# The first eight heads of a hybrid decoder block with queries on partitions, on one core

## The chip, the core and the metric

The kernel runs on one core of a Trainium2 chip. The core has five engines that each work through a queue of their own in order: TensorE (PE: matrix products, with a separate row PEld for loading its stationary operand), VectorE (DVE), ScalarE (ACT), GpSimd (POOL) and SyncE (SP), which here only issues transfers. The transfers of all queues run on 16 DMA engines. SBUF has 128 partitions; TensorE writes to PSUM, which has eight banks of 128 x 512 float32. The metric is the time of one execution on the device in microseconds.

## The reference, cut to what is computed

One decoder layer over 2048 tokens of width 1024, all in float32. A projection of the normed input gives queries, keys and values of eight heads of 64, and two halves u and v of a gated unit. Attention mixes three causal patterns (window, dilation), merged by their softmax denominators:

```python
DILATED_PATTERNS = ((128, 1), (512, 4), (2048, 16))
q, k, v_a, u, v_s = jnp.split(rms_norm(x, pre_mix_norm) @ w_in, ...)
for window, dilation in DILATED_PATTERNS:
    o, lse = dilated_window_attention(q, k, v, window, dilation)   # softmax over keys t - j*dilation
o = sum(softmax(lses)[p] * outs[p])                                # the three patterns merged
sgu = gelu(u) * (tril(w_spatial) @ layer_norm(gelu(v_s)) + b)      # per chunk of 128 tokens and group of 64
y = concat(rms_norm(attn), rms_norm(sgu)) @ w_out
x = x + rms_norm(y);  x = x + rms_norm(swiglu_ffn(rms_norm(x)))
```

## The kernel before

Float32 products are made of three (or two) products of halves: each operand is split into a rounded part (`hi`, a cast on ScalarE) and the rest (`lo`, a subtraction on VectorE). The 2048 tokens are four blocks m of 512. Attention runs in two halves x = 0, 1 of 1024 query tokens, eight heads each ("the first eight heads" are the eight heads of x = 0). Work is written as Python generators whose steps are interleaved by `_merge` (L1265) at a fixed pace; from that program order, with priority offsets (`high_priority`), a scheduler with its own model of times fixes the order of each engine's queue and each wait when the kernel is built. Buffers come from pools: tiles with one tag share `bufs` slots, and a new tile waits until the last reader of the old one is done.

Stages, in order: input projection of keys, queries and values of blocks 0 and 1 (to 187 us in the trace); then `merge(w1, ..., heads(0), ...)` at L1357 runs the rest of the input projection (gated unit of blocks 0 and 1, all of blocks 2 and 3) beside the heads of x = 0 (to 693 us); then output projection and the first FFN beside the heads of x = 1 (to about 1500 us); then the rest.

Attention, as it is before for both halves. `stacks` (L554) loads queries and keys of a head, transposed (dims on partitions, hi and lo rows stacked) and copies the keys of the near pattern on GpSimd to another order. `scores` (L652) computes scores with keys on partitions and up to 512 (key block, query) columns per PSUM bank; the scores go through `psq`, a pool of two banks (L107) that the gating product, the transposes of the gated unit and of the input preparation use as well. VectorE adds a mask whose values also carry the multiplicity of patterns (L723, L725, L733), and `fold` keeps a running maximum `macc` over keys. When all eight banks of a head are done, `lanes` (L599) transposes `macc` in 32 x 32 blocks, reduces it and `mix` (L740) spreads it back over the partitions as `mb`. Then each bank gets a subtraction of `mb` (L806, L811), an exponential on ScalarE (L819), the split into `ph` and `pl` (L820, L821), a running sum `dacc`, and products with the values into two accumulating banks per pattern kind (`psv`, L796, L798). At the end `lanes` reduces `dacc`, its reciprocal goes through DRAM (`dd`) and comes back spread over partitions (`rb`), and the pair of heads is divided (L852) and stored in `aT`. The scores of the next head are interleaved with `mix` of this one.

`ip_again` (L384) loads the normed input of block 0 again on SP. `ip_gate` (L499) loads the split gating weights (`ws`, 1 MB) once per block, four times in all. `out_rows` (L873) ends an output projection: after the last bank it loads eight rows of tiles of the residual (`xr`, one tile in the stage beside the heads of x = 1), adds each, stores it, takes its square on ScalarE, and fetches the next `xr` into the tile just freed:

```python
        def row(i, r):                                            # L895
            v.scalar_tensor_tensor(yj, yj, r, xs[i], ALU.mult, ALU.add)
            self.dma(dst[j * P:(j + 1) * P, 512 * n:512 * n + 512], yj)
            fetch(i + ahead)
```

Of the kernel before, what the change touches and what calls it, by code (L numbers as in the profile page):

```python
# [10 lines left out]
F32 = mybir.dt.float32  # L11
# [36 lines left out]
def shape_constants():  # L48
    i = np.arange(P)
    d = i[None, :] - i[:, None]  # L50
    ln2 = 8.0 * np.log(2.0)

    def logmul(dl):
        m = ((dl >= 0) & (dl <= 128)).astype(int) + ((dl >= 0) & (dl % 4 == 0)).astype(int)
        return np.where(m == 0, NEG, np.where(m == 1, 0.0, ln2))

    m0, m1, m2 = (logmul(d + 128 * k) for k in range(3))
    q = np.arange(256)
    r, nq, ii = q // 64, (q // 32) % 2, q % 32
# [5 lines left out]
    fcol = np.repeat(freq, 16)[:, None]  # L65
    return np.ascontiguousarray(
        np.concatenate([m2, m2, m1, m2, m0, m0, m1, p1, tril, fcol], axis=1).astype(np.float32))

# [9 lines left out]
SU_AT = 1  # L78
XR = 1
PV_LAG = 1  # L80
GATE_LAG = 1
PV_BUF = 3
R1 = 1.2
R2 = 1.1
# [11 lines left out]
C_FREQ = 1280  # L96
C_W = 1281


class Body:  # L100
# [32 lines left out]
    def dma(self, out, in_):  # L133
        if out.dtype == F32R:
            out = out.bitcast(F32)
        if in_.dtype == F32R:
            in_ = in_.bitcast(F32)
        self.nc.sync.dma_start(out, in_)  # L138

    def rstd(self, ss, n, inv_n, eps, name, parts=P):  # L140
# [358 lines left out]
    def ip_gate(self, m):  # L499
# [49 lines left out]
    def attn_pools(self, pool):  # L549
        self.ap = pool  # L550
        self.cst = pool.tile([P, C_TRIL], F32, name="cst")
        self.dma(self.cst, self.t["consts"][:, 0:C_TRIL])
# [46 lines left out]
    def lanes(self, acc, op, name):  # L599
# [3 lines left out]
        oth = self.tiny.tile([P, 32], F32, name=name + "_o", tag="ln_o", bufs=2)  # L603
        tr = self.ap.tile([P, 1024], F32, name=name + "_t", tag="mt", bufs=1)
        v.transpose(tr, acc)
# [260 lines left out]


    def ff_pools(self, pool, apool, ypool, xr):


        self.fp, self.fa, self.yp, self.xr = pool, apool, ypool, xr

    def out_rows(self, m, n_k, load, ops, res, gain, dst, keep):  # L873
# [12 lines left out]
        todo = [(n, j) for n in range(2) for j in range(4)]  # L886
        ahead = self.xr[2]

# [43 lines left out]
    def out_proj(self, m):  # L932
        nc, t, v, pool = self.nc, self.t, self.nc.vector, self.fp
        ah = [self.fa.tile([P, TB], F32R, name="ah", tag="ah", bufs=KT) for _ in range(KT)]
        al = [self.fa.tile([P, TB], F32R, name="al", tag="al", bufs=KT) for _ in range(KT)]
        rb = pool.tile([P, TB], F32, name="rbw", tag="tmp", bufs=4)
        order = [4, 5, 6, 7, 0, 1, 2, 3]
        with self.tc.high_priority(HP_O):
            for kt in order:
                raw = pool.tile([P, TB], F32, name="araw", tag="tmp", bufs=4)  # L940
                if kt < 4:
# [29 lines left out]
    def ffn_up(self, m):  # L971
# [5 lines left out]
        for g in range(NFF // 2):  # L977
# [17 lines left out]
            def evac(b, ps, g=g, hold=hold):  # L995
                if b < 2:
                    s = pool.tile([P, TB], F32, name="sil", tag="tmp", bufs=4)
                    nc.scalar.activation(s, ps, AF.Silu)
# [17 lines left out]
    def ffn_down(self, m):  # L1016
# [4 lines left out]
        def load_d(k, n):  # L1021
            s = pool.tile([P, TB], F32, name="araw", tag="tmp", bufs=4)
            self.dma(s, self.fD[m][k])
# [280 lines left out]
def build(tc, t):  # L1304
    with ExitStack() as ctx:
# [5 lines left out]
        with tc.tile_pool(name="sp", bufs=1, side="right") as sp:  # L1311
# [12 lines left out]
            with tc.tile_pool(name="su2", bufs=1) as su:  # L1324
# [4 lines left out]
                         36))  # L1329
        atx = ExitStack()  # L1330
        at = atx.enter_context(tc.tile_pool(name="at", bufs=1, side="right"))
        b.attn_pools(at)
        b.sbufs = 12
        ssq = at.tile([P, 1024], F32, name="ssq")
        b.ssq = [ssq, ssq]

        def heads(x):
            st, pair = {}, {}
            yield from b.scores(x, 0, st)
            for h in range(NH):  # L1340
# [6 lines left out]
                for _ in ahead:  # L1347
                    yield
            yield from b.attn_norm(x)

        G = 8 + 2 * GATE_LAG
        g0 = b.ip_gate(0)
# [3 lines left out]
                   _merge(b.ip_qkv(3), 30, b.ip_gate(3), 2 * G))  # L1356
        merge(w1, 4 * 50 + 24 + 4 * G, heads(0), 175 * R1)  # L1357
        ipx.close()
        ffx, fax = ExitStack(), ExitStack()
        ff = ffx.enter_context(tc.tile_pool(name="ff", bufs=1, side="left"))  # L1360
        fa = fax.enter_context(tc.tile_pool(name="fa", bufs=1, side="left"))
        b.ff_pools(ff, fa, ff, (ff, "xr", 1))
        merge(chain(b.out_proj(0), b.out_proj(1), b.ffn_prep(0), b.ffn_up(0),
                    _merge(b.ffn_down(0), 49, b.ffn_prep(1), 12), b.ffn_up(1)), 269, heads(1), (8 * 29 + 1) * R2)
        atx.close()
        with tc.tile_pool(name="ob", bufs=1, side="right") as ob:
            b.ff_pools(ff, fa, ff, (ob, "xr", 8))
            drain(b.out_proj(2))
            b.ff_pools(ff, ob, ob, (ob, "xr", 8))
            drain(b.out_proj(3))  # L1370
# [3 lines left out]
        b.hp = hpx.enter_context(tc.tile_pool(name="hp", bufs=1, side="right"))  # L1374
        b.ff_pools(ff, None, ff, (ff, "tmp", 4))
        with tc.tile_pool(name="pp", bufs=1, side="right") as pp:
# [40 lines left out]
```

## Time and profile before

Three runs took 2468.97, 2476.92 and 2474.16 us, median 2474.16. The profiled execution took 2476.58 us; its span from the first to the last instruction is 2474.8 us at a mean granted TensorE clock of 0.963 of full speed.

| engine | busy us | share of the span | instructions |
|---|---|---|---|
| PE | 2281.4 | 92% | 10421 |
| PEld | 1863.8 | 75% | 10421 |
| DVE | 1770.1 | 72% | 3430 |
| ACT | 1169.1 | 47% | 2141 |
| POOL | 349.3 | 14% | 373 |

All 347,600 packets of data went through one queue, that of SP (474.76 MB). Busy shares are unions of the instructions' spans, so two that overlap count once; in groups by line the spans are added. "granted clock" is the share of the full 2.4 GHz that TensorE was given; 0.5 is its lower level of 1.2 GHz. Matmuls are pipelined: the spans of neighbours overlap, and the distance from start to start is what one costs.

### The profile page before, as it was taken

What the parts mean: (1) busy time and instruction counts of PE and PEld (TensorE: products, weight loads), DVE (VectorE), ACT (ScalarE), POOL (GpSimd) and SP (SyncE); (2) the same over time, 40 slices, a digit from 0 to 9 for tenths busy, and PEclk for the clock granted to TensorE, in tenths of its full rate; (3) what the DMA queues carried; (4) which work ended last, traced back from release to release, by engine and by line L of the source; (5) the groups of instructions that cost most, each with busy time, mean ns of one, the idle gap of its engine ahead of it and who ended that gap; (6) DMA issues with size and microseconds to landing.
All of it is one profiled execution on the core that took longest, in us unless ns stands there. A gap on an engine that the chain in (4) does not pass through costs nothing. (4 is left out here: it accounts for less than half of the span.)

```text
span 2474.8 us, 32763 instructions
## 1 busy us (share of the span) xinstructions
PE 2281.4 (92%) x10421; PEld 1863.8 (75%) x10421; DVE 1770.1 (72%) x3430; ACT 1169.1 (47%) x2141; POOL 349.3 (14%) x373
## 2 busy tenths in 40 slices
PE   7997969889886999999999999999979999999997
PEld 6776758768675878887777888787757778887886
DVE  5428678995799985868899734667767676675567
ACT  6425765664644653535545532555422233334443
POOL 0000000000000000000000000000054466561012
PEclk9998979999998999999999999999989999999999
DMA  7867767778776665446656435678466633326655
GB/s 233 303 211 255 222 188 221 233 230 245 245 229 198 180 186 151 137 145 207 204 160 195 134 112 161 216 230 264 148 213 228 210 107 107 107 98 217 204 175 199
DMA packets 347772, 476.84 MB, mean 193 GB/s; under 512 B 30768, under 2 KB 174672, under 8 KB 347088
## 3 DMA queue, kind: packets, MB, share of 16 engines
q1 hardware_dynamic: 347600, 474.76, 60.5%
q8 instruction: 82, 1.34, 0.2%
q14 instruction: 90, 0.74, 0.1%
HBM read 365.12 MB, written 109.52 MB: 192 GB/s over the span
## 5 line engine op out<-in xcount | busy, mean ns | idle before, releaser
L171 DVE TENSOR_TENSOR w_lo<-w_raw,w_hi 128x512 fp32r<-128x512 f32 x368 | 252.6, 689 | 178.1 <-ACT w_hi L170 169.7
L170 ACT CAST w_hi<-w_raw 128x512 fp32r<-128x512 f32 x368 | 227.1, 618 | 307.1 <-PE d L199 236.2
L199 PE MATMUL d<-al,w_hi 128*128 128x512 f32 x704 | 276.4, 393 | 0.0
L199 PE MATMUL d<-ah,w_hi 128*128 128x512 f32 x704 | 276.3, 393 | 0.0
L199 PE MATMUL d<-ah,w_lo 128*128 128x512 f32 x704 | 276.1, 392 | 0.0
L1160 PE MATMUL d<-th,w_lo 128*128 128x512 f32 x616 | 246.6, 400 | 18.8 <-DVE w_lo L1047 18.7
L1160 PE MATMUL d<-th,w_hi 128*128 128x512 f32 x616 | 246.9, 401 | 11.4 <-ACT w_hi L1046 11.4
L1160 PE MATMUL d<-tl,w_hi 128*128 128x512 f32 x616 | 246.9, 401 | 0.0
L1047 DVE TENSOR_TENSOR w_lo<-raw,w_hi 128x512 fp32r<-128x512 f32 x187 | 142.6, 802 | 68.8 <-ACT w_hi L1046 67.8
L1046 ACT CAST w_hi<-raw 128x512 fp32r<-128x512 f32 x187 | 107.0, 618 | 131.8 <-PE d L1246 78.4
L199 PE MATMUL d<-w_hi,hh 128*128 128x512 f32 x384 | 153.7, 407 | 9.3 <-DVE io L436 4.8
L1160 PEld LDWEIGHTS d<-th,w_lo 128*128 128x128 f32 x616 | 118.4, 192 | 51.5 <-DVE w_lo L1047 25.3
L199 PE MATMUL d<-w_lo,hh 128*128 128x512 f32 x384 | 154.2, 402 | 2.5 <-DVE w_lo L171 2.2
L199 PE MATMUL d<-w_hi,hl 128*128 128x512 f32 x384 | 152.6, 400 | 0.0
L199 PEld LDWEIGHTS d<-ah,w_lo 128*128 128x128 f32 x704 | 132.7, 188 | 26.3
L199 PEld LDWEIGHTS d<-al,w_hi 128*128 128x128 f32 x704 | 132.7, 188 | 25.8
L199 PEld LDWEIGHTS d<-ah,w_hi 128*128 128x128 f32 x704 | 132.7, 189 | 25.0
L818 POOL MEMSET ph<- 128x128 f32 x64 | 13.1, 205 | 978.1 <-PE pv L796 611.1
L1160 PEld LDWEIGHTS d<-th,w_hi 128*128 128x128 f32 x616 | 118.6, 193 | 39.5 <-ACT w_hi L1046 12.9
L199 PE MATMUL d<-w_hi,fh 128*128 128x512 f32 x352 | 140.3, 398 | 4.1 <-ACT fh L1013 3.8
L199 PE MATMUL d<-w_hi,fl 128*128 128x512 f32 x352 | 138.2, 395 | 1.9 <-DVE fl L1014 1.9
L1160 PEld LDWEIGHTS d<-tl,w_hi 128*128 128x128 f32 x616 | 119.1, 193 | 25.1
(283 smaller groups left out, 5608.8 us busy)
## 6 DMA issues: line engine op xcount, KB each, us to landing
w_raw<-in_w_in SPq DMA_DIRECT2D x136, 256.0 KB
w_lo<-wc SPq DMA_DIRECT2D x96, 256.0 KB
w_raw<-in_w_gate SPq DMA_DIRECT2D x88, 256.0 KB
w_raw<-in_w_up SPq DMA_DIRECT2D x88, 256.0 KB
w_raw<-in_w_down SPq DMA_DIRECT2D x88, 256.0 KB
araw<-fD SPq DMA_DIRECT2D x88, 256.0 KB
raw<-fS SPq DMA_DIRECT2D x77, 256.0 KB
w_raw<-in_w_out SPq DMA_DIRECT2D x64, 256.0 KB
```

The lines of the kernel that those rows point to most:

```text
L170: nc.scalar.copy(hv, rv)
L171: nc.vector.tensor_tensor(lv, rv, hv.bitcast(F32), ALU.subtract)
L199: nc.tensor.matmul(banks[b], lhsT, rhs, start=(k == 0 and j == 0), stop=(k == nk - 1 and j == len(ops) - 1))
L818: nc.gpsimd.memset(t[:, :o].bitcast(F32), 0.0)
L1046: nc.scalar.copy(hv, src)
L1047: nc.vector.tensor_tensor(lv, src, hv.bitcast(F32), ALU.subtract)
L1160: nc.tensor.matmul(ps, a[:, c], b, start=(k == 0 and n == 0), stop=(k == 3 and n == 2))
```

## The change

For x = 0 the heads are written anew (`tq_*`); x = 1 keeps the old code. Scores are computed with queries on partitions (stationary operand: queries; moving: keys). A head has eight banks of up to 512 columns: four of the strided pattern pair (one per residue r, a block of 128 and one of 256 keys) and four of the near pattern (two query blocks each). For each query block one VectorE instruction adds the mask, scales by -1/8 and keeps the minimum over keys in a column of `M`; the exponential takes that column as bias per partition and sums itself into a column of `D`. TensorE then transposes the weights block by block into a bank of the same pool `psq`, from where ScalarE and VectorE split them into `ph` and `pl`; products with the values follow as before, on halves of a head's result that are copied out as soon as each is complete. The strided and the near part are normalized separately; per pair of heads `tq_merge` brings minima and sums through DRAM into one order, computes both parts' weights on 32 partitions, and brings these back spread over the partitions. Its transfers go by `put`, that is GpSimd's queue, as do the reloads of `ip_again`. The copies on GpSimd are now of queries (`q1`). The gating weights are loaded once and kept in the pool of x = 0. That pool is closed and a new one opened before the heads of x = 1. The first head starts before six steps of `w1`, and the pace is 133 x 1.25 steps instead of 175 x 1.2. In `out_rows` beside x = 1, `xr` takes slots of the shared tag `tmp` (five slots instead of four), and three rows are fetched ahead instead of one.

```diff
-R1 = 1.2
+T_BUF = 5
+HEAD_AT = 6
+T_LAG = 2
+T_END = 3
+HP_T = 200
+HP_S = 0
+R0 = 1.25
+    def put(self, out, in_):
...
+        self.nc.gpsimd.dma_start(out, in_)
@@ ip_again
-                self.dma(h[i][k], self.hD[k, i])
+                self.put(h[i][k], self.hD[k, i])
@@ ip_gate
-        ws = pool.tile([P, 2, 8, P], F32R, name="ws", tag="big", bufs=4)
-        self.dma(ws, self.wsD)
+        ws = self.ws
+    def tq_near(self, x, h, ld):
...
+        for src in ld[:2]:
+            d = pool.tile([P, 8, P], F32R, name="q1", tag="q1", bufs=2)
+            for mm in range(2):
+                nc.gpsimd.tensor_copy(...)
+    def tq_scores(self, x, ld, units, md, h2):
+        ps = self.psq.tile([P, 512], F32, name="qk", tag="qk")
+        s = pool.tile([P, 512], F32, name="S", tag="S", bufs=T_LAG + 4)
...
+                for o, rhs in prods:
+                    nc.tensor.matmul(o, left[0], rhs, start=True, stop=False)
+                    nc.tensor.matmul(o, left[1], rhs, start=False, stop=True)
...
+        for off, w, mask, c in todo:
+            so = s[:, off:off + w]
+            with self.tc.high_priority(HP_E):
+                v.tensor_tensor_reduce(out=so, in0=ps[:, off:off + w], in1=mask, scale=-0.125, scalar=BIG, op0=ALU.add,
+                                       op1=ALU.min, accum_out=M[:, c:c + 1])
+            nc.scalar.activation(so, so, AF.Exp, scale=-1.0, bias=M[:, c:c + 1], accum_out=D[:, c:c + 1])
+    def tq_turn(self, x, units, s, ld):
...
+        tp = self.psq.tile([P, 512], F32, name="qk", tag="qk")
+        with self.tc.high_priority(HP_T):
+            for src, dst in blocks:
+                i = s[:, src * P:(src + 1) * P]
+                if isinstance(dst, int):
+                    nc.tensor.transpose(tp[:, dst * P:(dst + 1) * P], i, self.ident)
...
+            nc.scalar.copy(ph[:, :w], tp[:, :w])
+            v.tensor_tensor(pl[:, :w], tp[:, :w], ph[:, :w].bitcast(F32), ALU.subtract)
+    def tq_heads(self, x):
...
+        for i in range(n):
+            h, b = divmod(i, nb)
+            todo = self.tq_turn(x, banks[b], weights.pop(i), loads[h])
+            late.append((i, todo))
+            if len(late) > PV_LAG:
+                pv(*late.pop(0), acc)
+            yield
+            if i + T_LAG < n:
+                a_step(i + T_LAG)
+                yield
+            if i >= PV_LAG and (i - PV_LAG) % (2 * nb) == 2 * nb - 1:
+                wait.append([T_END, self.tq_merge(x, (i - PV_LAG) // (2 * nb), stat, outs)])
...
+    def tq_merge(self, x, pr, stat, outs):
+        v.transpose(T[:, 0, :], M)
+        v.transpose(T[:, 1, :], D)
+        self.put(rr, T.rearrange("p s i -> p (s i)"))
+        self.put(C[:, 1], rv[1])
+        for a in range(4):
+            self.put(C[8 * a:8 * a + 8, 0], rn[0, a])
+        yield
...
+        for a in range(4):
+            self.put(ww.rearrange(...)[a], W[8 * a:8 * a + 8]...)
+        for t in range(2):
+            for h2 in range(2):
+                self.put(wb[1 - t][64 * h2:64 * h2 + 64]..., ww[t, h2].partition_broadcast(64))
+        yield
+        for half in range(2):
+            z = slice(2 * half, 2 * half + 2)
+            v.tensor_tensor(a1[:, z], a1[:, z], wb[0][:, z], ALU.mult)
+            v.tensor_tensor(un[:, z], un[:, z], wb[1][:, z], ALU.mult)
+        for mm in range(2):
+            v.tensor_tensor(at[:, c]..., un[:, :, mm, :], a1[:, :, mm, :], ALU.add)
+            self.dma(self.aT[2 * x + mm][pr], at[:, c])
...
@@ out_rows
-        ahead = self.xr[2]
+        ahead = self.xr[3]
@@ build
+        atx = attn(0, lambda pool: b.tq_pools(0, pool))
...
-        merge(w1, 4 * 50 + 24 + 4 * G, heads(0), 175 * R1)
+        first = tq_heads(0)
+        next(first)
+        drain(islice(w1, HEAD_AT))
+        merge(w1, 4 * 50 + 24 + 4 * G - HEAD_AT, first, 133 * R0)
+        atx.close()
+        atx = attn(1, b.attn_pools)
...
-        b.ff_pools(ff, fa, ff, (ff, "xr", 1))
+        b.ff_pools(ff, fa, ff, (ff, "tmp", T_BUF, 3))
```

## Rows read from the trace of the kernel before

**Rows 1.** Busy time by stage: start:end us, length, engines (xcount), clock, DMA, GB/s

```profile
187.00:693.00 506.00, 428.33 (x2066) 352.16 (x2065) 394.46 (x957) 307.60 (x584) 24.47 (x79) 0.92 0.74 231
693.00:800.00 107.00, 85.18 (x404) 69.74 (x403) 98.92 (x217) 48.73 (x96) 5.61 (x14) 0.90 0.65 204
800.00:1500.00 700.00, 676.57 (x3242) 559.37 (x3243) 548.96 (x1164) 351.14 (x594) 18.44 (x69) 0.99 0.55 165
```

**Rows 2.** The same view (PE, PEld, DVE, ACT, POOL), three stretches inside the first stage

```profile
205.00:220.00 15.00, 4.85 (x20) 3.68 (x21) 14.17 (x41) 6.03 (x11) 1.97 (x1) 0.84 0.66 179
320.00:350.00 30.00, 12.71 (x51) 10.41 (x50) 23.11 (x69) 16.08 (x34) 1.57 (x4) 0.56 0.65 185
400.00:650.00 250.00, 226.76 (x1117) 187.10 (x1116) 195.62 (x454) 155.40 (x294) 11.10 (x40) 0.97 0.77 242
```

**Rows 3.** Timeline of VectorE, 327 to 336: start us, us, instruction, out and in

```profile
327.69 1.23 DVE L605 STREAM_TRANSPOSE mx_t<-macc 128x1024 f32<-128x1024 f32 x1
...
331.94 1.24 DVE L749 STREAM_TRANSPOSE mb<-mx_r 128x1024 f32<-128x1024 f32 x1
```

**Rows 4.** Busy time (DVE, ACT) of tile macc, dacc, then mb, 187 to 693

```profile
187.00:693.00 506.00, 47.95 (x113) 9.16 (x32) 0.92 0.74 231
187.00:693.00 506.00, 45.01 (x104) 9.64 (x32) 0.92 0.74 231
187.00:693.00 506.00, 53.64 (x136) 0.92 0.74 231
```

**Rows 5.** Groups by line on VectorE, 187 to 693: xcount | busy us, mean ns | idle

```profile
L723 DVE TENSOR_TENSOR S<-qk,cst 128x384 f32<-128x384 f32 (+1 forms) x39 | 21.8, 565 | 17.4 <-PE qk L716 17.1
L725 DVE TENSOR_TENSOR S<-qk,cst 128x512 f32<-128x512 f32 x24 | 16.4, 685 | 3.1 <-PE qk L716 3.0
L733 DVE TENSOR_TENSOR S<-qk,cst 128x256 f32<-128x256 f32 x8 | 3.3, 408 | 4.3 <-PE qk L716 4.3
```

**Rows 6.** Groups by line and shape on ScalarE, 187 to 693

```profile
L819 ACT ACTIVATE S<-S 128x384 f32<-128x384 f32 x40 | 20.5, 523 | 13.9 <-DVE S L811 13.8
L819 ACT ACTIVATE S<-S 128x512 f32<-128x512 f32 x24 | 14.9, 627 | 3.1 <-DVE S L811 3.0
L525 ACT ACTIVATION_READ_ACCUMULATOR junk<-ug 128x1 f32 x16 | 3.1, 196 | 0.0
```

**Rows 7.** Timeline of TensorE at 517.5 to 519: transposes, then products with values

```profile
517.55 0.60 PE L323 MATMUL qk<-ident,xs 128*128 128x128 f32 x4
517.91 0.36 PE L796 MATMUL pv<-ph,v 128*128 128x256 f32 x1
518.11 0.28 PE L798 MATMUL pv<-pl,v 128*128 128x256 f32 x1
518.23 0.28 PE L796 MATMUL pv<-ph,v 128*128 128x256 f32 x1
...
518.47 0.39 PE L796 MATMUL pv<-ph,v 128*128 128x128 f32 x2
...
518.92 0.22 PE L796 MATMUL pv<-ph,v 128*128 128x128 f32 x1
```

**Rows 8.** Transfers, 187 to 693: packets, bytes, mean rate

```profile
DMA packets 87578, 117.03 MB, mean 231 GB/s; under 512 B 8120, under 2 KB 40888, under 8 KB 87028
```

**Rows 9.** Timelines of SP and VectorE: denominator to DRAM, spread again, first use

```profile
660.55 1.24 SPq L138 DMA_DIRECT2D dd<-dn_w  x1
...
669.32 2.05 DVE L852 TENSOR_TENSOR at<-at,rb 128x512 f32<-128x512 f32 x2 [3.47 <-DMA rb<-dd]
```

**Rows 10.** Timeline of VectorE in 755 to 803: two of eight row sums

```profile
763.54 0.75 DVE L898 SCALAR_TENSOR_TENSOR y<-y,po_y,xr 128x512 f32<-128x512 f32 x1 [0.65 <-DMA xr<-in_x]
...
770.01 0.75 DVE L898 SCALAR_TENSOR_TENSOR y<-y,po_y,xr 128x512 f32<-128x512 f32 x1 [1.22 <-DMA xr<-in_x]
```

**Rows 11.** Timelines of TensorE and VectorE: one bank of scores filled and read

```profile
527.24 0.39 PE L715 MATMUL qk<-qs,k 128*128 128x256 f32 x1 [1.45 <-DVE S L725]
...
528.09 0.69 DVE L725 TENSOR_TENSOR S<-qk,cst 128x512 f32<-128x512 f32 x1
```

More of the change, by code (lines that the diff above doesn't have):

```diff
@@ L865, in attn_norm, with tq_pools, tq_load, rows @@
         yield
+    def tq_pools(self, x, pool):
+        self.ap, self.lt = pool, "at"
+        if x == 0:
+            self.ws = pool.tile([P, 2, 8, P], F32R, name="wgt")
+            self.dma(self.ws, self.wsD)
+        self.tq = pool.tile([P, C_END - C_T4], F32, name="cstq")
+        self.dma(self.tq, self.t["consts"][:, C_T4:C_END])
+    def tq_load(self, x, h):
+        nc, pool = self.nc, self.ap
+        nkm = 2 * (x + 1)
+        def rows(scr):
+            return scr.rearrange("(a h d) t -> h a d t", a=8, h=8)[h]
+        qs = pool.tile([P, 4, 2, P], F32R, name="qs", tag="qs", bufs=1)
+        ql = pool.tile([P, 4, 2, P], F32R, name="ql", tag="ql", bufs=1)
+        ks = pool.tile([P, nkm, TB], F32R, name="ks", tag="ks", bufs=2)
+        for mm in range(2):
+            q = self.qT[2 * x + mm]
+            for dst, src in ((qs[0:64], q[0]), (qs[64:128], q[0]), (ql[0:64], q[1]), (ql[64:128], q[1])):
+                self.dma(dst[:, :, mm, :], rows(src))
+        for m in range(nkm):
+            for s in range(2):
+                self.dma(ks[64 * s:64 * s + 64, m, :], rows(self.kT[m][s]))
+        return [qs, ql, None, ks, None, None]
@@ new lines, in tq_near @@
+    def tq_near(self, x, h, ld):
+        nc, pool = self.nc, self.ap
+        nkm = 2 * (x + 1)
+        ld[2] = []
+        for src in ld[:2]:
+            d = pool.tile([P, 8, P], F32R, name="q1", tag="q1", bufs=2)
+            for mm in range(2):
+                nc.gpsimd.tensor_copy(d[:, 4 * mm:4 * mm + 4, :].rearrange("p j (r i) -> p j r i", r=4),
+                                      src[:, :, mm, :].rearrange("p r (j i) -> p j r i", j=4))
+            ld[2].append(d)
+        v4 = [pool.tile([P, 4, P], F32R, name="v4", tag="v4", bufs=4) for _ in range(nkm)]
+        n0 = 0 if x == 0 else 7
+        v1t = pool.tile([P, 8 * (x + 1) - n0, P], F32R, name="v1", tag="v1", bufs=2 - x)
+        for m in range(nkm):
+            self.dma(v4[m].rearrange("p r d -> p (r d)"), self.vD[m][h].rearrange("(i r) d -> i (r d)", r=4))
+            lo = max(n0, 4 * m)
+            cnt = 4 * m + 4 - lo
+            if cnt > 0:
+                src = self.vD[m][h].rearrange("(j i r) d -> r i j d", r=4, i=32)
+                for r in range(4):
+                    self.dma(v1t[32 * r:32 * r + 32, lo - n0:lo - n0 + cnt, :], src[r, :, 4 - cnt:4])
+        ld[4:] = v4, {n: v1t[:, n - n0, :] for n in range(n0, 8 * (x + 1))}
@@ L935, in out_proj @@
         al = [self.fa.tile([P, TB], F32R, name="al", tag="al", bufs=KT) for _ in range(KT)]
-        rb = pool.tile([P, TB], F32, name="rbw", tag="tmp", bufs=4)
+        rb = pool.tile([P, TB], F32, name="rbw", tag="tmp", bufs=T_BUF)
         order = [4, 5, 6, 7, 0, 1, 2, 3]
@@ L939, in out_proj @@
             for kt in order:
-                raw = pool.tile([P, TB], F32, name="araw", tag="tmp", bufs=4)
+                raw = pool.tile([P, TB], F32, name="araw", tag="tmp", bufs=T_BUF)
                 if kt < 4:
@@ L996, in evac @@
                 if b < 2:
-                    s = pool.tile([P, TB], F32, name="sil", tag="tmp", bufs=4)
+                    s = pool.tile([P, TB], F32, name="sil", tag="tmp", bufs=T_BUF)
                     nc.scalar.activation(s, ps, AF.Silu)
@@ L1021, in load_d @@
         def load_d(k, n):
-            s = pool.tile([P, TB], F32, name="araw", tag="tmp", bufs=4)
+            s = pool.tile([P, TB], F32, name="araw", tag="tmp", bufs=T_BUF)
             self.dma(s, self.fD[m][k])
@@ L1329, in build, with attn, tq_heads @@
                          36))
[L1330 to L1335, printed above, removed]
+        def attn(x, setup):
+            atx = ExitStack()
+            at = atx.enter_context(tc.tile_pool(name="at", bufs=1, side="right"))
+            setup(at)
+            b.ssq = [at.tile([P, 1024], F32, name="ssq")] * 2
+            return atx
+        def tq_heads(x):
+            yield from b.tq_heads(x)
+            yield from b.attn_norm(x)
         def heads(x):
```

216 lines of the change are left out of this document (209 added, 7 removed).

## The prediction

> **What bounds the kernel now.** I read the busy shares of the page first: TensorE 92%, VectorE 72%, ScalarE 47%, so TensorE is the bound on average. Then the table of stages [rows 1], because the diff rewrites only the stage in which the first eight heads share the engines with the rest of the input projection, 187 to 693 us. The reader is to see that TensorE is much less full there than later: 428.3 us of 506 at a granted clock of 0.92, against 676.6 of 700 at 0.99 from 800 on. In full-clock terms 428.3 x 0.92 = 394 us of work fill 506 us, a rate of 0.779; from 800 to 1500 it is 676.6 x 0.99 / 700 = 0.957. So some 110 us of this stage are not matrix work: 77.7 us idle, the rest a lower clock. VectorE (394.5 us) is 78% busy, ScalarE 61%, DMA 74%.
>
> Where does the loss sit? The table of shorter stretches [rows 2] shows two dips: 205 to 220 has 4.9 us of TensorE in 15, 320 to 350 has 12.7 in 30 at clock 0.56 (mostly the 1.2 GHz level, after an idle stretch). In the first VectorE is busy for 14.2 of 15 us. The undisturbed 400 to 650 runs at 226.8 x 0.97 / 250 = 0.88. VectorE's order of time in the second dip [rows 3] says what it does: from 327.7 to 333.2 us it turns the running maximum of a head across partitions and spreads it again, and only then can the first exponential of that head, its casts and its products with V follow. The same turn stands at the end of each head for the denominator. TensorE has products with V in its queue and stands in order behind them. That is the bound of the dips: a serial VectorE chain at a head's boundary, in a stage where VectorE has little slack.
>
> **The change, part by part.** The sum is made against the profiled execution (span 2474.8 us, time 2476.6 us), 0.1% above the median of 2474.2.
>
> *Softmax per query row.* With queries on partitions, the maximum comes out of the mask addition and the sum out of the exponential, per bank, and the head-wide chain goes. Removed on VectorE: everything on the running maximum, the running sum and the spread maximum, 47.95 + 45.01 + 53.64 = 146.6 us [rows 4], with 18.8 us of ScalarE copies. The mask additions, 21.8 + 16.4 + 3.3 = 41.5 us [rows 5], become 128 additions with a minimum (per head 11 of 256 columns and 5 of 128). No row shows such an instruction: not below 41.5, since the columns are the same; above, a separate read of the minimum, priced as ScalarE's read of a sum, 0.196 us [rows 6], on top of 0.408: 77. I take 0.408 each, 52, from the plain addition of the same tile. The merge adds per pair of heads four 512-column multiplications (0.685), two strided additions (1.03, as the old division in [rows 9]) and a dozen small ones, each under 0.408: at most 9.7 us, 39 for four pairs, against 8 us of old division. VectorE: -146.6 + 11 + 39 - 8 = -105, so about 290 us.
>
> ScalarE: exponentials were 40 x 0.523 + 24 x 0.627 = 36 us. From these two sizes a column costs 0.81 ns, so 88 of 256 columns and 40 of 128 cost 0.419 and 0.315, together 49.5, and 128 reads of sums 25.1 [rows 6]. Minus the copies: +20, to 327 us, 69% of the new stage. It is hidden as long as no burst meets the GELU evictions; if that cover goes, a part of the 20 us shows.
>
> TensorE: per head 64 products of 256 columns and 6 of 128 become 36 and 36. From start to start one of 256 costs 0.12 us; four of 128 start from 518.47 to 518.92, so 0.11 each, hardly less [rows 7]: 8.3 us before and after. New are 27 transposes per head: four start over 0.36 us in that row and span 0.60, so 0.09 to 0.15 each; I take 0.11, 3.0 us. Each bank's transposes also break the stream, and the first product after a change of kind takes 0.20 instead of 0.12: 16 more runs, 1.3 us. Net +4.3 per head, +34 us (24 to 47) on the engine that bounds, and it hides behind nothing.
>
> Stage: 394 + 34 = 428 us of full-clock work. The rate of 400 to 650 is 0.88 with VectorE at 78%; with VectorE near 61% and no head boundary I take 0.90 for the whole stage: 428 / 0.90 = 476, a gain of 30 us. Own range: rate 0.86 to 0.93, 498 to 460, a gain of 8 to 46.
>
> *Gating weights kept, reload and merge on GpSimd's queue.* Three loads of 1 MB and eight broadcasts of 256 KB leave, sixteen broadcasts of 256 KB come: 117 MB [rows 8] become about 116. SP loses 16 reloads, 3 weight loads and 16 of the old division. The one weight load left, 1 MB or 4.5 us at 231 GB/s, stands ahead of the first queries on SP; six projection steps that go first cover it. On GpSimd's queue a merge now has four transfers in series, with the copies of the next head's queries queued behind whatever waits there. In the trace two such steps in series, from SP, took 660.55 to 669.32, 8.8 us [rows 9]; four take 17.6 if GpSimd's cost the same (bounds: the 8.8 of two, and twice the 17.6). A pair has 16 bank steps of some 6 us, and the merge starts three steps late, so I cost it at nothing; without that cover it is 17.6 us once, after the last pair, and there input projection is still running (130 attention steps at a pace of 133 x 1.25 to 258 end at 130 / 166 = 78% of it). The copies wait at most for the same 17 us, and their products come four banks, 24 us, later.
> GpSimd issues no transfer in this trace; the Trainium skill (DMA: Bandwidth & Descriptors, "Anatomy of one DMA — SWDGE (gpsimd) path") prices one from that queue at about 2.0 us plus its bytes over 436 GB/s, an estimate of 8 to 10 us for the chain, by which the sum stays the same.
>
> *Rows through three tiles.* In the output projection under the second eight heads, each row waits for the row before to free the one tile: two sums start 6.5 us apart for 0.75 us of work, with a wait of 1.2 us on VectorE [rows 10]. Three tiles let them follow in about a third. TensorE loses 22 us in 693 to 800 [rows 1], with VectorE 92% busy there, so most of that is VectorE. Against it the second eight heads now wait for the first heads' pool and reload their masks. Bounds -15 and +10; I take -5.
>
> Sum: 2476.6 - 30 - 5 = 2441, and 0.1% lower for the median: 2439.
>
> **Rivals.**
> *Near-continuous TensorE.* If VectorE caused nearly all of the loss, the stage runs at the 0.957 of 800 to 1500: 428 / 0.957 = 447, 59 us less, with the rows about 2410. For it: the dips. Against: DMA is busier here (74% against 55%), and the two scratch banks are used more.
> *Transfers take over.* 116 MB must still come in. At the 231 GB/s of [rows 8] the stage lasts 502 us, at the 242 of 400 to 650 [rows 2] 479: 2443 to 2470. For it: 74% mean DMA share. Against: the same row of 400 to 650 has 77% with TensorE 91% busy.
> *The two scratch banks decide (slower).* Scores, gating and preparation share two PSUM banks: 64 + 32 + 16 = 112 fills in the stage. Transposed weights now go there as well: 176. A scores bank is held from its first matmul at 527.24 until the addition ends at 528.78, 1.5 us [rows 11]; a transposed one for four transposes, a copy and a subtraction of 512 columns in series, 0.44 + 0.63 + 0.69 = 1.76 us [rows 5 to 7], and queueing. At 2.5 us each the banks are busy for 176 x 2.5 / 2 = 220 us, no bound. It decides from 176 x h / 2 = 506, h = 5.75 us, on: at 6 us the stage is 528, +22, and the time 2496. Each step now also has two passes through ScalarE and VectorE with TensorE between, in an in-order queue, so h can grow.
> The Trainium skill (Perfetto Trace Analysis, "Matmuls") says that matmul groups should rotate through different PSUM banks so that evictions overlap the next group's matmuls, and prefers larger matmuls; this change does the opposite in both. By that rule the time is this rival's. The trace so far bears it out little: the addition of [rows 11] starts 0.85 us after its first matmul, so little queues there, but with 112 fills.
> *The dips are not VectorE's (slower).* If the loss of 110 us comes from the order of loads and queues, it stays, and the +34 us of TensorE come on top: up to 2506, at the least no change. Against it: VectorE is 94% busy in the first dip.
>
> **How the numbers follow.** Chances: forecast 0.47 (2423 to 2461), near-continuous 0.15, transfers 0.15, banks 0.11, dips not VectorE's 0.12. A measurement of this kernel can tell 0.3%, 7.4 us, from no change. Faster: 0.47 + 0.15 + 0.11 of the transfers = 0.73. Slower: the banks' 0.11 and 0.08 of the last = 0.19. Same: 0.04 + 0.04 = 0.08. The range 2400 to 2494 leaves out about 0.05 below and 0.14 above.
>
> **What would show it.** Right: no running maximum or sum in the first stage, VectorE near 290 us there, no dip of TensorE of over 8 us before 500, granted clock at 0.95 or more, about 216 added transposes of 0.11 us, stage end near 660. Each step: the minimum's additions near 0.41 us for 256 columns; exponentials with reads of 0.2 us; sums of rows 2 to 3 us apart. Wrong: TensorE waits before transposes or scores for ScalarE and VectorE on the shared banks of several us in sum per head; weight waits on DMA; a gap where the second eight heads begin; or a VectorE instruction with minimum of more than 0.6 us.

## The result, and the profile after

The changed kernel took 2514.34 us (median of 4 runs, 2509.69 to 2520.53) beside 2475.54 us of the kernel before on the same chip: ratio 1.0158, 95% interval 1.0133 to 1.0182. It is slower by 39 us, where 35 less was forecast, and 20 us above the end of the range. Its profiled span is 2510.6 us, 35.8 above the span before.

Two marks cut both spans into three parts: the start of the last product of `w_lo` with `hh` (end of the input projection) and the start of the second transposition of `ssq` (end of the second eight heads).

| us | to the end of the projection | from there to the end of the second heads | the rest |
|---|---|---|---|
| before | 680.3 | 811.4 | 983.1 |
| after | 708.9 | 816.5 | 985.2 |
| difference | +28.6 | +5.1 | +2.1 |

Busy time by stretch (start:end, length, PE, PEld, DVE, ACT, POOL with counts, clock, DMA share, GB/s). First the kernel before, to the mark of the table instead of the 693 of [rows 1]:

```profile
187.00:681.00 494.00, 421.73 (x2040) 346.64 (x2038) 384.22 (x925) 303.78 (x576) 24.47 (x79) 0.92 0.74 230
```

Then the changed kernel; the first row answers to [rows 1], the others to [rows 2]:

```profile
187.00:709.00 522.00, 450.87 (x2302) 366.20 (x2302) 249.37 (x704) 320.62 (x713) 59.17 (x104) 0.95 0.71 212
205.00:220.00 15.00, 14.49 (x72) 11.46 (x71) 11.59 (x37) 14.39 (x35) 2.94 (x6) 1.00 0.71 203
320.00:350.00 30.00, 16.66 (x80) 13.73 (x80) 12.71 (x51) 20.30 (x49) 5.36 (x10) 0.71 0.63 163
400.00:650.00 250.00, 221.46 (x1168) 182.55 (x1166) 121.40 (x330) 151.55 (x340) 26.20 (x45) 0.97 0.70 207
```

TensorE's work is 450.87 x 0.95 = 428 us at full clock, the number that was forecast; to the same mark it was 421.73 x 0.92 = 388 before, so some 40 us were added. (Busy time times a mean clock printed with two digits is good to a few us.) VectorE fell to 249 us, further than the 290 forecast, ScalarE rose to 321. But 71 us of the stage are still idle on TensorE (494 - 422 = 72 before, to the same mark). The dip at 205 is gone; the one at 320 is there again with VectorE idle for most of it; and 400 to 650, which was undisturbed before, runs at 221.46 x 0.97 / 250 = 0.86 with VectorE 49% busy, where [rows 2] give 0.88 with 78%. So less load on VectorE did not by itself make that stretch faster; the merges, new in it, have their share in this (`a_nomerge` below).

Part of the dip at 320 is the first merge: without its exchange 5.8 of the dip's 13.3 us of idle time are gone (`a_nomerge` below). First VectorE's order of time (start, duration, in brackets the idle time before and what ended it), then TensorE's:

```profile
312.25 0.20 DVE L1151 STREAM_TRANSPOSE tqT<-tqD 128x32 f32<-128x32 f32 x1
...
314.80 0.56 DVE L1030 TENSOR_TENSOR pl<-qk,ph 128x384 fp32r<-128x384 f32 x1 [0.31 <-ACT ph L1029]
323.61 0.21 DVE L1165 TENSOR_TENSOR tqm<-tqC 32x64 f32<-32x64 f32 x1 [8.25 <-DMA tqC<-rr]
323.85 0.35 DVE L1167 TENSOR_TENSOR tqW<-tqm,tqC 32x64 f32<-32x64 f32 x2
324.13 0.27 DVE L988 CUSTOM_DVE_ANT_0 S<-qk,cstq 128x128 f32<-128x128 f32 x1
...
336.65 0.34 DVE L1174 TENSOR_TENSOR tqW<-tqW,tqm 32x64 f32<-32x64 f32 x2
...
349.78 1.29 DVE L1189 TENSOR_TENSOR un<-un,wn 128x512 f32<-128x512 f32 x2 [6.10 <-DMA wn<-ww]
350.99 0.75 DVE L349 SCALAR_TENSOR_TENSOR hl<-qk,gT,hh 128x512 fp32r<-128x512 f32 x1
```

```profile
324.90 0.55 PE L536 MATMUL qk<-vh,wgt 128*128 128x256 f32 x1 [5.69 <-DVE tqM L988]
...
344.49 0.48 PE L556 MATMUL qk<-ident,ug 128*128 128x128 f32 x1 [5.75 <-ACT ug L550]
...
351.79 0.48 PE L346 MATMUL qk<-ident,xs 128*128 128x128 f32 x1 [1.70 <-DVE hl L349]
```

VectorE stands 8.25 us before a small instruction on the two parts' minima, because these are still on their way through DRAM. Behind it in the queue is the score addition of L988 that empties a scratch bank; TensorE's gating product wants that bank and waits 5.69 us, to 324.90. From 343.7 on VectorE stands for 6.10 us before the multiplication with `wn`; behind that is the split `hl` (L349), for which TensorE waits 1.70 us, to 351.79. The wait of 5.75 us to 344.49 is another: it began before VectorE stood there, and what it waits for is the gated unit on ScalarE (L550). Over the stage VectorE waits like this for 18.3 + 27.7 us:

```profile
DVE un L1189 <- DMA wn<-ww: 27.7, 3, 13.5
DVE tqm L1165 <- DMA tqC<-rr: 18.3, 4, 8.2
```

At the seam, TensorE, and SP beside it:

```profile
709.10 0.39 PE L222 MATMUL d<-w_hi,hl 128*128 128x512 f32 x1
722.20 0.79 PE L222 MATMUL d<-w_hi,ah 128*128 128x512 f32 x1 [12.71 <-DMA araw<-sT]
...
732.26 0.55 PE L737 MATMUL qk<-qs,ks 128*128 128x256 f32 x1 [5.62 <-DMA ks<-kT]
```

```profile
699.32 0.33 SPq L153 DMA_DIRECT2D cst<-consts  x1
...
726.29 4.86 SPq L153 DMA_DIRECT2D ks<-kT  x8
```

The last projection product starts at 709.10, the output projection at 722.20, the first scores of the second heads at 732.26, because their keys are fetched only from 726.29 on. Before, those scores ran ahead of the projection's end:

```profile
676.29 0.50 PE L715 MATMUL qk<-qs,ks 128*128 128x256 f32 x2 [0.84 <-DMA qs<-qT]
```

The rows of the output projection, to be held against the 6.5 us of [rows 10]:

```profile
802.65 3.39 DVE L1233 SCALAR_TENSOR_TENSOR y<-y,po_y,xr 128x512 f32<-128x512 f32 x5
810.11 0.75 DVE L1233 SCALAR_TENSOR_TENSOR y<-y,po_y,xr 128x512 f32<-128x512 f32 x1 [0.88 <-DMA xr<-in_x]
```

Eight of them take 11.7 us from 802.65 to 814.3, against 42 us before (757.65 to 799.94).

### The profile page after: what moved, and what is told of

Same layout as the page of the kernel before. It is cut to its first block, busy times and chain, and to the rows that moved or that the text cites. A ratio compares the mean times of both kernels' runs of the same rounds, so it can differ in the third digit from the quotient of the medians.

```text
span 2510.6 us, 33239 instructions
## 1 busy us (share of the span) xinstructions
PE 2308.4 (92%) x10685; PEld 1881.7 (75%) x10685; DVE 1633.2 (65%) x3202; ACT 1190.5 (47%) x2282; POOL 385.6 (15%) x397
## 5 line engine op out<-in xcount | busy, mean ns | idle before, releaser
L222 PE MATMUL d<-w_lo,fh 128*128 128x512 f32 x352 | 137.5, 391 | 0.0
```

The source lines that it names most:

```text
L222: nc.tensor.matmul(banks[b], lhsT, rhs, start=(k == 0 and j == 0), stop=(k == nk - 1 and j == len(ops) - 1))
```

## The experiments

Theories: **W**, the added matrix work costs what it weighs and the idle time stays; **B**, the shared scratch banks hold TensorE; **S**, the seam between the two pools; **Q** and **M**, the merge's trips, above all from GpSimd's queue; and the prediction's own step, that VectorE holds the stage. Each was timed against the kernel before. "Projection" is the start of its last product and "second heads" the time from there to their end, as in the table above (680.3 and 811.4 before, 708.9 and 816.5 after). The kernel before took a median of 2471 to 2476 us beside these runs, so a difference between two of the kernels below is good to some 4 us.

**Without the transposes.** `a_noturn`:

```diff
-        tp = self.psq.tile([P, 512], F32, name="qk", tag="qk")
-        with self.tc.high_priority(HP_T):
-            for src, dst in blocks: ...transpose...
+        tp = s
```

> The changed kernel without its 216 transposes and without the 64 scratch banks they fill: the split into ph and pl reads the exponentials from SBUF as they are (so the products with V get weights that are not transposed). Theory W (the added matrix work costs what it weighs, idle time of TensorE stays): 48.7 us of transposes go, at clock 0.95 some 46 us: about 2468, idle of TensorE in 187 to the first output projection still near 70 us. Rival B (the two shared scratch banks and the second pass through ScalarE and VectorE hold TensorE up): idle falls as well, by 20 us or more: 2445 or below.

2471.22 us, ratio 0.9992 (0.9973 to 1.0011): 43 us less than the changed kernel, W's number. Projection 676.3, second heads 813.2.

```profile
187.00:676.70 489.70, 422.67 (x2073) 347.08 (x2071) 249.62 (x705) 320.85 (x713) 58.99 (x101) 0.93 0.75 225
```

Work is 422.67 x 0.93 = 393 us, 35 less than the 428: 0.16 us for each of the 216 transposes, with what they break up. Idle time is 67 us, hardly less than 71 though 64 of 176 bank fills are gone. That is W, not B.

**Transposes twice.** `a_turn2`: `for src, dst in blocks + blocks:`.

> The changed kernel with each transpose issued twice into the same place, so 216 more transposes and no further bank, copy or subtraction. Theory W: about +46 us, 2560. Rival B: TensorE has slack of about 70 us in the stage, and only the hold of 64 banks grows, by 0.44 us each over two banks, 14 us: about 2528.

2524.68 us, ratio 1.0206 (1.0177 to 1.0235): only 10 more than the changed kernel, 35 below W's number and 3 below B's. Projection 721.5, second heads 814.1.

```profile
187.00:721.90 534.90, 468.62 (x2499) 388.47 (x2499) 246.76 (x703) 320.90 (x711) 57.88 (x100) 0.95 0.69 205
```

Work is 445 us, 17 more, so a repeated transpose costs about 0.08 us. My 46 came from summed spans of a group in which neighbours overlap (48.7 us for the 216). At the right price W gives 17 and B its 14; the stage grew by 12.6, with 66 us idle. So this run does not tell them apart, though B's number came; `a_noturn` does.

**The pool reopened, alone, on the kernel before.** `b_reopen`:

```diff
         merge(w1, 4 * 50 + 24 + 4 * G, heads(0), 175 * R1)
+        atx.close()
+        atx = attn()
```

> The kernel before with one edit: the attention pool is closed after the first eight heads and opened anew for the second eight, masks loaded again. Theory S (a good part of the loss is the seam at 700 to 740, because the second heads' tiles wait for the first heads' pool): +8 to +20 us against before, 2484 to 2496, with a gap of TensorE of 10 us or more where the second heads begin. Against it (the seam is only where the later end of the first heads shows): within 4 us of before.

2492.77 us, ratio 1.0081 (1.0057 to 1.0106): 20 us slower, S. Projection 673.0 (7 earlier, why is open), second heads 833.9 (22 longer). TensorE's largest waits there, where before it had scores to compute:

```profile
PE d L199 <- ACT ah L951: 17.5, 1, 17.5
PE d L199 <- DVE y L907: 14.3, 1, 14.3
```

**No maximum, no sum, on the kernel before.** `b_nofold`, for x = 0:

```diff
-            self.fold(us, s, macc, ALU.max, seen)
+            if x:
+                self.fold(us, s, macc, ALU.max, seen)
... the same for lanes, mb, the subtraction of mb, dacc and its lanes
```

> The kernel before without the running maximum, the subtraction of the maximum and the running sum in the first eight heads (the weights there are not normalized), so that VectorE has some 150 us less in the first stage and TensorE the same work. The prediction's step (VectorE's load and head boundaries hold the rate at 0.78; without them 0.90): the stage falls from 506 to about 438 us, 2408. Theory W (idle is mostly made by chains over several engines and transfers, VectorE's share being the boundary dips alone): 12 to 30 us less, 2446 to 2464.

2453.00 us, ratio 0.9926 (0.9902 to 0.9950): 21 us less, W's range and a third of what the prediction's step says. Projection 655.9, second heads 806.0.

```profile
187.00:656.30 469.30, 415.53 (x2043) 342.30 (x2041) 235.97 (x472) 286.63 (x511) 27.65 (x85) 0.94 0.75 238
```

With 148 us less on VectorE, TensorE's 391 us of work take 469, a rate of 0.83. Idle falls from 72 to 54, what the clock takes from 34 to 25. That is all that this work of VectorE was worth. And it sat where the prediction saw it: the two dips of [rows 2] had 10 + 17 = 27 us of TensorE idle, and now have

```profile
205.00:220.00 15.00, 10.81 (x53) 8.95 (x53) 12.27 (x26) 9.95 (x17) 2.14 (x8) 0.87 0.67 203
320.00:350.00 30.00, 24.69 (x112) 19.28 (x111) 17.15 (x38) 24.04 (x46) 1.23 (x6) 0.68 0.58 159
```

4.2 + 5.3 = 9.5 us: that is the 18 by which the idle time of the stage fell. The idle time outside the dips, 45 us before, is 44.

**Second heads' tiles in a pool of their own.** `a_seam`:

```diff
+        b.xp = xpx.enter_context(tc.tile_pool(name="xp", bufs=1, side="right"))
+        self.cst = self.xp.tile([P, C_TRIL], F32, name="cst")      # loaded at the start
-        qs = pool.tile(...); ql = pool.tile(...); ks = pool.tile(...)   # both halves
+        qs = self.xp.tile(...); ql = self.xp.tile(...); ks = self.xp.tile(...)
-        s = pool.tile([P, 512], F32, name="S", tag="S", bufs=T_LAG + 4)
+        s = pool.tile([P, 512], F32, name="S", tag="S", bufs=T_LAG + 3)
```

> The changed kernel with masks, queries and keys of the second eight heads in a pool of their own that outlives the first heads' pool (masks loaded at the start; queries and keys take the slots of the first heads' as these come free), and one score tile less for the first heads to make room. Theory S (the seam costs some 20 us of the loss, as the reopened pool alone did): the second heads start 15 us or more earlier, the gap after the projection shrinks, 2494 to 2504. Against it (other tiles of the old pool, or the operands of the output projection, come later than the masks anyway): within 5 us of the changed kernel, 2509 to 2519.

The edit also moves the load of the gating weights from the start to the first gate. 2497.40 us, ratio 1.0098 (1.0073 to 1.0123): 17 less (15 by the ratios), S. Projection 712.1, 3 later, second heads 797.5, 19 less.

**Other pace.** `a_pace16`: `R0 = 1.6` for 1.25.

> The changed kernel with the first heads paced at 133 x 1.6 steps instead of 133 x 1.25, so that they should end earlier against the projection. Theory S: the pool comes free and the attention's output stands ready before the projection ends, so the gap at the seam goes: 8 to 15 us less, about 2502. Theory W alone (the same matrix work, idle made by chains): within 5 us of 2514, or slower if attention steps closer together wait more for ScalarE and VectorE.

2502.96 us, ratio 1.0113 (1.0095 to 1.0131): 11 less, S again. Projection 708.4 as before the edit, second heads 806.7: all of it is the seam.

**Transfers from SP.** `a_spqueue`:

```diff
-        self.nc.gpsimd.dma_start(out, in_)
+        self.nc.sync.dma_start(out, in_)
```

> The changed kernel with the merge's transfers and the reload of block 0 issued from SP instead of GpSimd; nothing else. Theory Q (GpSimd's queue, with landings of 5 to 7 us and copies of queries behind it, feeds the waits of the stage): 5 to 15 us less, about 2504. Rival (the merge has its cover, and on SP weights would queue behind it): 0 to 10 us more, 2514 to 2524.

2492.85 us, ratio 1.0070 (1.0054 to 1.0086): 21 less, somewhat beyond Q's range. Projection 693.8, second heads 813.8: 15 of it in the first stage.

```profile
187.00:694.20 507.20, 449.33 (x2305) 366.78 (x2303) 248.66 (x704) 316.31 (x710) 21.63 (x32) 0.96 0.72 219
```

```profile
DVE un L1189 <- DMA wn<-ww: 14.8, 2, 10.0
DVE tqm L1165 <- DMA tqC<-rr: 10.1, 3, 8.0
```

Same work (431), idle 58 instead of 71, and VectorE's two waits nearly halved.

**Rows through three tiles, alone, on the kernel before.** `b_rows3`:

```diff
-... tag="tmp", bufs=4        b.ff_pools(ff, fa, ff, (ff, "xr", 1))
+... tag="tmp", bufs=5        b.ff_pools(ff, fa, ff, (ff, "tmp", 5, 3))
-        ahead = self.xr[2]
+        ahead = self.xr[3]
```

> The kernel before with the rows of the output projection in the shared tag, five slots instead of four and three rows ahead instead of one; nothing else. The prediction's step: 5 us less, about 2469, with the sums of two rows 2 to 3 us apart. Rival (the second heads' work covers the rows): within 4 us of before.

2459.63 us, ratio 0.9933 (0.9906 to 0.9959): 15 us less, three times the forecast of this part. Projection 681.7, second heads 796.3, 15 less.

```profile
755.71 3.39 DVE L898 SCALAR_TENSOR_TENSOR y<-y,po_y,xr 128x512 f32<-128x512 f32 x5
762.56 0.75 DVE L898 SCALAR_TENSOR_TENSOR y<-y,po_y,xr 128x512 f32<-128x512 f32 x1 [0.61 <-DMA xr<-in_x]
```

**Only the reload from SP.** `a_spreload`: `self.dma` for `self.put` in `ip_again`.

> The changed kernel with only the reload of block 0 (16 transfers) issued from SP; the merge's transfers stay on GpSimd. The same edit together with the merge gave 21 us. Theory M (it is the merge: VectorE waits in order for its two trips through DRAM, and these land later from GpSimd): at most 5 us less, 2509 to 2516. Rival L (it is the reload: the projection that follows waits for it, and copies of queries stand behind it): 13 to 22 us less, 2492 to 2501.

2516.93 us, ratio 1.0168 (1.0147 to 1.0189): nothing gained, M. So by difference it is the merge; its transfers alone were not moved.

**The exchange left out.** `a_nomerge`: `T`, `rr`, `C`, `W`, `E`, `ww` and their transfers go; `ws` and `wn` are filled with a constant on GpSimd.

> The changed kernel without the exchange in the merge: minima and sums stay where they are, 14 transfers, 2 transposes and a dozen small VectorE instructions per pair of heads are left out, and both parts are multiplied by constants; the reload stays on GpSimd. Theory M: VectorE's 46 us of waits for tqC and wn go, 18 us less or more, 2496 or below. Rival L: only the instructions themselves count, 0 to 6 us less, 2508 to 2516.

2480.27 us, ratio 1.0022 (1.0003 to 1.0040): 34 less, M. Projection 684.6, second heads 810.4.

```profile
187.00:685.00 498.00, 447.68 (x2295) 368.76 (x2293) 242.77 (x669) 320.68 (x709) 34.36 (x52) 0.95 0.70 215
```

Idle is 50 us: 21 of the 71 belonged to the exchange, though its instructions are only 7 us of VectorE's busy time. In the same run, the stage to 400, the stretch of [rows 2] after it, and the dip:

```profile
187.00:400.00 213.00, 185.52 (x960) 151.66 (x959) 109.36 (x325) 151.36 (x347) 22.91 (x36) 0.93 0.71 214
400.00:650.00 250.00, 231.18 (x1214) 192.84 (x1214) 123.88 (x331) 158.76 (x346) 11.45 (x16) 0.97 0.69 213
320.00:350.00 30.00, 22.50 (x105) 19.18 (x106) 17.53 (x52) 24.46 (x58) 1.35 (x2) 0.66 0.49 152
```

Without the exchange 400 to 650 runs at 231.18 x 0.97 / 250 = 0.90 instead of 0.86, and the dip at 320 has 7.5 us idle instead of 13.3. What stands before 400 runs at 0.81.

**Three repairs at once.** `a_all`: `a_seam`, `a_spqueue` and `a_pace16` together.

> The changed kernel with three repairs at once: second heads' masks, queries and keys in a pool of their own, merge and reload issued from SP, first heads paced at 133 x 1.6. Alone they gave 17, 21 and 11 us. If the seam and the queue are separate causes, the first two add (38 us) and the pace adds little to the seam's repair (0 to 6 us): 2470 to 2478, the time of the kernel before, since the transposes stay. If they repair one and the same wait: 2485 to 2493.

2476.85 us, ratio 1.0010 (0.9998 to 1.0021): 38 less, as the queue and the seam add up to; the causes are separate, and the pace adds nothing to the seam's repair. Projection 700.0, second heads 794.3.

**Which wait of the merge?** `a_tend1`: `T_END = 1`. `a_gap2`: the same, and `w[0] = 2` after each part.

> The changed kernel with the merge started two bank steps earlier (T_END 1 instead of 3), its three parts still one step apart. Theory P (results of the next pair wait for a1 and un, which have one buffer each, until the merge is through): 8 us less or more, up to 2506. Theory V (VectorE, working in order, comes to a merge instruction before its transfer has landed, and what TensorE needs stands behind it): within 5 us of the changed kernel, since the parts follow each other as closely as before.

> As the one with the earlier start, and the merge's three parts two bank steps apart instead of one; transfers stay on GpSimd. Theory V: VectorE's waits for tqC and wn (46 us in the stage) fall below 20, 10 to 25 us less than the changed kernel, 2489 to 2504. Theory P: no better than the earlier start alone, or worse, since a1 and un are held longer.

2516.35 us (1.0172, 1.0149 to 1.0196) and 2510.63 us (1.0154, 1.0125 to 1.0183). V had named the first number, and the second is nearer to P's, but neither run decides: the first merge starts 3 to 4 us earlier, and the scheduler that fixes the queues put its two waiting instructions behind the same neighbours in VectorE's queue as before, so the waits stayed. Of `a_gap2`:

```profile
DVE un L1190 <- DMA wn<-ww: 30.0, 3, 14.5
DVE tqm L1166 <- DMA tqC<-rr: 18.7, 4, 8.1
```

**The same on top of the repairs.** `a_all1`.

> The three repairs together (2476.9) with the merge started earlier and its parts two steps apart. If VectorE's waits are what is left of the merge's cost (34 us without the exchange, of which the queue's change gave 21): 5 to 13 us less, 2464 to 2472. If SP had already covered them: 2474 to 2480.

2473.60 us, ratio 1.0005 (0.9987 to 1.0022): 3 us less than `a_all`, between the two expectations and within what can be told apart.

**The merge's arithmetic on GpSimd.** `a_pool`: `nc.gpsimd.tensor_tensor` for `v.tensor_tensor` in `tq_merge`, the reciprocal stays. `a_all_pool`: the same on `a_all`.

> The changed kernel with the merge's arithmetic moved from VectorE to GpSimd (the mean of the two minima takes the place of the smaller one, to the same result); only the reciprocal stays on VectorE; transfers stay on GpSimd's queue. Theory V (what costs is that VectorE stands in order before tqC and wn, with score and weight instructions behind it): VectorE's waits for tqC and wn, 46 us, go to GpSimd, and the time falls by 10 to 25 us, 2489 to 2504. Theory P (the next pair's results wait for a1 and un until the merge is through): GpSimd is slower at it, so a1 and un come free later: 2514 or more.

> The three repairs together (2476.9) with the merge's arithmetic on GpSimd. Theory V: VectorE's remaining waits for the merge (14 us) and its 25 us of work go: 5 to 12 us less, 2465 to 2472. Theory P: 2477 or more.

2515.54 us (1.0158, 1.0131 to 1.0185) and 2483.29 us (1.0036, 1.0022 to 1.0049): no gain, and 6 us lost, P's number both times. But the edit did not free VectorE: the waits for `tqC` and `wn` left it, and others came in their place (`a_pool`):

```profile
DVE tqm L1174 <- POOL tqm L1173: 22.7, 4, 10.3
DVE ssq L1201 <- ACT a L1200: 19.5, 3, 9.1
```

VectorE now stands before the reciprocal and the last sum of squares. TensorE also waited 6.2 us once for a result of the next pair, whose copy on ScalarE waited 8.2 us for `at` (the one buffer of `a1`, P). So V and P are not told apart: in these traces an instruction of the merge that VectorE or ScalarE reaches too early passes the length of the trip on, whichever it is.

**Pace on the kernel before with the rows.** `b_rows3p`: `R1 = 1.4` for 1.2.

> The kernel before with the rows through three tiles (2459.6) and the first heads paced at 175 x 1.4 instead of 175 x 1.2. The pace helped the changed kernel by 11 us at the seam; the pool is not reopened here, so the seam's theory gives 0 to 4 us less, 2455 to 2460. If attention steps closer together wait more for VectorE, which is 78% busy there: 3 to 10 us more.

2470.07 us, ratio 0.9997 (0.9977 to 1.0018): 10 us above `b_rows3` (16 by the ratios), at or beyond the upper end of the second expectation. The projection ends at 688.2 instead of 681.7.

The fastest version that computes the whole layer is `b_rows3`, the kernel before with one part of the change: 2459.63 us, below both kernels.

## Why the prediction was wrong, step by step

*TensorE's work: right.* 428 us forecast, 428 measured; 216 transposes, 35 us with what they break up (forecast 34 with the changes of kind). That the two sums agree so closely is luck: the forecast's 394 runs to 693, past the mark, and to the mark some 40 us were added, within the 24 to 47 forecast. Nothing hides it: without the transposes the kernel is 43 us faster.

*"With VectorE near 61% and no head boundary I take 0.90 for the whole stage": this is the step that failed.* The stage ran at 428 / 522 = 0.82. It was to lose 64 of its 112 us of idle time and lower clock against 34 us of added work. To the mark, the work grew by 40, the idle time fell by 1 and what the clock takes by 11, so the stage became 28 us longer where 30 less was forecast. Of these 58 the exchange of the merge is 24 (next step); 34 remain without it: the stage is then 498 to the mark against 494 before, 4 longer instead of 30 shorter.

The 34 are nearly all the rate. The dips were read rightly: `b_nofold` takes VectorE's chain away and they shrink by 18 us. What failed is to carry this over to the whole stage. The dips held 27 of the 78 us of idle time. The 0.90, a step up from the 0.88 of 400 to 650, comes true in just that stretch (`a_nomerge`), while the whole stage reaches 0.83 in `b_nofold` and 447.68 x 0.95 / 498 = 0.85 in `a_nomerge`. At least 50 us of idle time remain in every variant. The waits of TensorE in the stage of the changed kernel name many short chains and no single engine: some 30 us on VectorE, 28 on ScalarE, 9 on transfers. The five longest (us, times, longest) are the gated unit twice, weights from DRAM, a scratch bank and the projections' evictions:

```profile
PE qk L556 <- ACT ug L550: 9.8, 5, 5.8
PE d L222 <- ACT ug L518: 8.1, 2, 6.7
PE d L222 <- DMA w_lo<-wc: 6.5, 8, 1.6
PE qk L536 <- DVE tqM L988: 6.5, 2, 5.7
PE d L222 <- DVE io L459: 6.0, 7, 1.2
```

The rival that the dips are not VectorE's was wrong about the dips, but right that most of the loss stays and the work comes on top; its 2506 was the nearest number.

*"I cost it at nothing" (the merge).* Without the exchange 34 us go, 24 of them in the stage. The trip is longer than the 17.6 us worked out: in the first merge 11.2 us from the end of the transposition of `D` (312.45) to the minima (323.61) and 12.8 from the weights (336.99) to the multiplication with `wn` (349.78), 24 in all; the small arithmetic between them takes 13.4 more, since it stands in the queues of VectorE and ScalarE among other work. What failed more is the cover. I looked at who needs the result (the copies of queries, the end of the pair) and not at who waits for it: the merge's instructions stand in the queues of VectorE and ScalarE, and scores and bank evictions behind them. The head-wide chain that was removed came back as one that goes through DRAM. The queue is 21 of the 34, as the difference of `a_spqueue` and `a_spreload`; whether by the landings or by the time that each issue takes on GpSimd is not split. Landings of the merge in the trace (KB each, median us from issue to landing):

```profile
wn<-ww POOLq DMA_DIRECT2D x8, 256.0 KB, 5.1
ws<-ww POOLq DMA_DIRECT2D x8, 256.0 KB, 7.5
tqC<-rr POOLq DMA_DIRECT2D x16, 4.0 KB, 4.0
```

As an estimate by the Trainium skill (DMA: Bandwidth & Descriptors, "Anatomy of one DMA — SWDGE (gpsimd) path") a landing takes 2.0 us for 4 KB and 2.6 us for 256 KB. The trace does not agree, it has twice that and more, and the trace decides.

*The rows and the seam: "I take -5".* Both signs were right and both sizes too small: the rows gave 15, the seam took 17 to 22 (bounds were -15 and +10), so the net is a loss of 2 to 7 where a gain of 5 was forecast. Both show singly, and 811.4 - 15 + 22 = 818 meets the 816.5 measured. I had named the gap as a sign of being wrong and priced it by its masks; what counts is that TensorE has scores to fill the wait for the output projection's operands only if the second heads' tiles can be loaded before the first heads are through.

*VectorE and ScalarE: right in kind.* The additions with a minimum take 419 ns for 256 columns, the read of the minimum 83 ns beside them; exponentials 502 and 400 ns instead of 419 and 315; whether these cost time was not tested.

```profile
L988 DVE CUSTOM_DVE_ANT_0 S<-qk,cstq 128x256 f32<-128x256 f32 x88 | 35.4, 419 | 29.6 <-PE qk L982 29.5
L988 DVE DVE_READ_ACCUMULATOR2_ANT tqM<- 128x1 f32 x128 | 10.6, 83 | 0.0
L990 ACT ACTIVATE S<-S,tqM 128x256 f32<-128x256 f32 x88 | 44.2, 502 | 8.6 <-DVE tqM L988 8.4
L990 ACT ACTIVATE S<-S,tqM 128x128 f32<-128x128 f32 x40 | 16.0, 400 | 20.5 <-DVE tqM L988 20.1
```

*The banks' rival: not it.* Idle fell by 4 us without the 64 added fills. But the two banks, with the fills that they had before, are where a wait of VectorE reaches TensorE (5.69 us at 324.90). *Transfers: not it.* The stage moved 212 GB/s, less than the 231 of [rows 8].

The single effects against the changed kernel or the one before (+43 transposes, +34 exchange, +17 seam, -21 the old running maximum and sum, -15 rows) sum to 58, not to 39: presumably they share waits, and no run here splits the remaining 19. What makes up the 50 us of idle time common to all variants, and what holds the stage before 400 at 0.81, stays open too.

## What to carry to other kernels

An engine that makes a dip is not yet the bound of the stage: add up how much idle time the dips hold, and take the engine's load away once (`b_nofold` was a few lines) before work is moved from it to the engine that is the bound. A chain through DRAM costs where its instructions stand in an in-order queue, so look at what stands behind each of them, not only at when its result is due. Tiles of the next stage must not lie in a pool that the last stage closes, if their work is what fills the seam.

## What the runs showed of the hardware

Issuing a transfer takes about 0.56 us on GpSimd's queue and about 0.30 us on SP's; the same 20 small loads in both queues (min/median/max ns, first and last start), first of the changed kernel, then of `a_spqueue`:

```profile
L161 POOL DMA_DIRECT2D tqC<-rr x20: 545/559/585, 318.3 to 654.8; - x20
```

```profile
L161 SPq DMA_DIRECT2D tqC<-rr x20: 284/299/2169, 310.4 to 644.7; - x20
```

An exponential with a bias per partition and a sum takes some 85 ns more at both sizes than the line through the two sizes of [rows 6], the read of the sum not counted. A transpose that repeats the run before it costs about half (0.08 us, `a_turn2`) of what the first run costs each with the products that it breaks up (0.16 us, `a_noturn`).
